# Starting addresses of the on-chip tiles in a two-block transformer kernel: transposed activations and weight buffers moved to multiples of 2048 bytes

## The chip, the cores and the metric

The kernel runs on one core of a Trainium2 chip. The metric is the device time of one execution in microseconds; three executions of the kernel before took 1178.62, 1178.98 and 1180.39 us (median 1178.98). The profile is that of one further execution, whose span from the first to the last instruction is 1177.9 us.

The engines are named as the profile names them: PE is the matrix engine (PEld its weight loads), DVE the vector engine, ACT the scalar engine, POOL GpSimd, SP the engine that issues most DMAs. In a matmul of this kernel the *stationary* operand is the activation tile (128 partitions x 128 columns, loaded before the matmul by a weight load) and the *moving* operand is a tile of weights (128 partitions x 512 columns, in some places 256) that streams past it.

## The reference, cut to what matters

Two transformer blocks in float32 over 256 tokens of width 1024: a first block of two layers (differential attention with a context, then multiscale pooling, each followed by a gated feed-forward net), and a second block (gated linear attention and block attention side by side, an MLP, a gated per-token embedding). Nearly all of the time goes to products of an activation by a weight matrix:

```
def swiglu(h, w_in, w_out):
    g, u = jnp.split(h @ w_in, 2, axis=-1)
    return (jax.nn.silu(g) * u) @ w_out
...
    h = rms_norm(x, norm_mix[i])
    u = h @ w_in[i]                                    # 1024 x 8208
    ...
    x = x + y @ w_out[i]
    h2 = rms_norm(x, norm_mlp[i])
    x = x + jnp.square(jax.nn.relu(h2 @ w_up[i])) @ w_down[i]
```

## The kernel before, in words

**Split products.** A product in float32 is made of three products in the matrix engine's one-pass format (float32r). An operand x is written as a rounded part `hi` and the rest `lo`; the product is act_hi x w_hi + act_hi x w_lo + act_lo x w_hi. So each weight block of 128 x 1024 float32 (`raw`, 512 KB, one DMA, L256) becomes two tiles: ACT writes `hi` (L286) and DVE writes `lo` = raw - hi (L292). Activations are kept transposed, k on the partitions, in two tiles each: `xTh`/`xTl` (128 x 8 x 256, the normalised input of every projection, of the gate and up products and of several output products), and others with the same role in places: `xa`/`s` (the context, k by 256 tokens), `hh`/`hl` (the hidden values of the feed-forward nets and the MLP, for the down products), `obT`/`qkd` (in the second block).

**The loops.** `mmN` (L377 to L379) runs a whole output tile of 128 tokens x 512 columns: for each of 8 k-steps three matmuls, hi x xTh, lo x xTh, hi x xTl, all into one bank. `mmK` (L391, L393) does the same for one k and two column halves, so each stationary tile meets two moving halves; `mmK_tail` (L404 to L406) is its last part. Some products stay in plain float32 (`raw` as the moving operand directly, for instance L385 and L497).

**What sets the order.** The order is written by hand, engine by engine. The class `Stream` walks one list of all weight blocks (`plan`): a DMA is issued as soon as one of the 8 `raw` buffers is free, a block is split into one of 8 `hi` and 8 `lo` buffers as soon as a pair is given back by `done`, and `done` is called when PE has used the block. Blocks of kind "m" in the same list are the 80 modulation blocks, which DVE alone reduces (L270).

**Where tiles lie.** A `Pool` hands out bytes in each partition in the order in which tile names are first asked for; pools that are opened later lie above. Pool `cp` is the lowest and holds, in this order, `prm` (parameters), `cst` (identity and tables), `xTh`, `xTl`, `mc0`, `mc1`, `half`, `crow`, and then small tiles; pool `rg` above it holds 8 `raw`, 8 `hi`, 8 `lo`; everything else is above `rg`. A tile's address therefore depends on the sizes of all tiles below it. PSUM tiles are in pool `pp` and are not touched.

Of the kernel before, what the change touches and what calls it, by code (L numbers as in the profile page):

```python
# [18 lines left out]
P = 128  # L19
# [144 lines left out]
CST_W = _o  # L164
# [9 lines left out]
def body(ctx: ExitStack, tc: tile.TileContext, wst, prm, cst, cst2, poolp, xT_d, cT_d, x_d, head, lam_d,  # L174
# [23 lines left out]
    cp = Pool("cp")  # L198
    ctx.callback(cp.close)
    rg = Pool("rg")  # L200
# [4 lines left out]
    def big():  # L205
        return pp.t([P, 1024], "big")
# [14 lines left out]
        return cp.t([P, w], f"st{w}", bufs=8)  # L221

    prm_s = cp.t([P, PRM_W], "prm")
    cst_s = cp.t([P, CST_W], "cst")
    xTh = cp.t([P, KD, T], "xTh", F32R)
    xTl = cp.t([P, KD, T], "xTl", F32R)
    mc = [cp.t([P, 48], f"mc{l}") for l in range(2)]
    half_e = cp.t([P, 8], "half")
    crow = cp.t([P, D], "crow")
    G.memset(half_e, -0.5)  # L230

    def prmc(n):
# [196 lines left out]
            A.activation(dh, ps, AF.Copy, scale=scale)  # L429
            V.scalar_tensor_tensor(dl, ps, scale, dh.bitcast(F32), op0=OP.mult, op1=OP.subtract)  # L430

    # ---------------------------------------------------------------- block 1, layer 0: projections
    b1 = Pool("b1")
    hch = b1.t([P, KD, T], "xa", F32R)
    hcl = b1.t([P, KD, T], "s", F32R)
# [215 lines left out]
            q_transposes(qr[tt - 2], tt - 2)  # L651
    a1.close()

    # ---------------------------------------------------------------- layer 0: differential attention
    a2 = Pool("a2")
    ss, ssum, ops, state, osb, rr = {}, {}, {}, {}, {}, {}

# [145 lines left out]
    for i in range(n_it + 5):  # L803
# [30 lines left out]
        if i >= 5 and items[i - 5][1] % 4 == 3:  # L834
            t, f = items[i - 5][0], items[i - 5][1] // 4
# [3 lines left out]
    a2.close()  # L839
    at.close()  # L840

    # ---------------------------------------------------------------- block 1: residual stream
    pw = []

    br = Pool("br")
# [231 lines left out]
    cur["grow"] = s[1]  # L1077
    linK8("WO", olh, wo_mid, core(0), wo_t0, core(1), wps[0])

    # ---------------------------------------------------------------- layer 0 ffn  # L1080
    nx = {}

    def mid_g2c():
# [57 lines left out]

    ffn(0, fp, x_t(1), ac0(0), mid_pool, ac0(1), {XM: mid_xa, 2: mid_g2c, 3: mid_g2r, 4: mid_gb, 5: mid_gbr})

    # ---------------------------------------------------------------- layer 1: multiscale pool
    pps = [big()]

    def res(t):
# [51 lines left out]
    st.hold = False  # L1199
    st.pump()  # L1200

    # ---------------------------------------------------------------- layer 1 ffn
    def mid1_c():
        nx["g2c"] = mcol(1, 5)
        nx["rows"] = ln_rows(3, 1.0)
# [34 lines left out]

    ffn(1, fp, x_t(1), ac1(0), lambda: None, after1_1, {XM: mid_xa, 4: mid1_c, 5: mid_g2r})

    # ---------------------------------------------------------------- block 2: projections
    hx.clear()
    state = {}
    fp.close()
# [59 lines left out]
        if i >= 2:  # L1306
            qk_tr()

    # ---------------------------------------------------------------- block 2: causal attention with distance bias
    mo_o = {}  # L1310
    mo_sum = {}
    mo_st = {}
# [60 lines left out]
    per = -(-len(steps) // 9)  # L1373
# [17 lines left out]
        steps.pop(0)()  # L1391
    mo.close()

    # ---------------------------------------------------------------- block 2: gated linear attention
    g2 = Pool("g2")
    obT = [g2.t([P, KD, T], f"obT{i}", F32R) for i in range(2)]
    for t in range(2):
# [131 lines left out]
    for i, (c, t) in enumerate(seq):  # L1529
        f = int(c[2])  # L1530
# [29 lines left out]
            g_fin(0)  # L1560
    g_fin(1)

    # ---------------------------------------------------------------- block 2: gated branches and output projection
    yT = [g2.t([P, KD, T], "obT0", F32R), g2.t([P, KD, T], "qkd", F32R)]
    for i, (f, t) in enumerate([(0, 0), (1, 0), (0, 1), (1, 1)]):
        sl = slice(512 * f, 512 * f + 512)
# [18 lines left out]
    gl.close()  # L1585
    fp = Pool("fp3")

    # ---------------------------------------------------------------- block 2: mlp
    J = DMLP // 512
    hs, hT = {}, {}  # L1590
    ops_ = [big(), big()]
# [58 lines left out]
            down(j, 1, True)  # L1650
            rcore(1)(ops_[1])

    # ---------------------------------------------------------------- block 2: gated per-token embedding
    st.hold = False
    st.pump()
    for i, (f, t) in enumerate([(0, 0), (1, 0), (0, 1), (1, 1)]):
# [117 lines left out]
```

## Time and profile before

| | before |
|---|---|
| median of 3 executions (range) | 1178.98 us (1178.62 to 1180.39) |
| span of the profiled execution | 1177.9 us |
| PE busy, share of the span | 1132.6 us, 96% |
| DVE busy | 761.6 us, 65% |
| ACT busy | 559.7 us, 48% |
| weights and inputs read | 232.63 MB, 198 GB/s over the span |

The busy time of PE is made of modelled matmul lengths, which overlap one another in time: a matmul of 512 columns is given some 390 to 400 ns, though the next one starts about 230 ns after it. The cost of a matmul in a dense run is therefore read from the distance between starts in the timeline, and the modelled length serves only to compare one group with another.

### The profile page before, as it was taken

The page shows a single profiled execution, that of the slowest core. Times are in us where ns is not written, and L with a number is a line of the kernel's source. Part 1 is how long each engine was busy: PE and PEld are TensorE (multiplying, and loading weights), DVE is VectorE, ACT ScalarE, POOL GpSimd, SP SyncE. Part 2 cuts the span into 40 slices and gives each one's busy share as a digit, 9 for nine tenths or more (in the row PEclk, how much of TensorE's full clock was granted, in tenths as well). Part 3 has the DMA queues.
Part 4 walks back from the last instruction along what each step waited for, and adds up shares of the span by engine and source line. Part 5 has one row for each costly group of instructions (what it writes and reads, how often), then busy time and mean ns, then how long its engine had stood idle before and what let it go on. Part 6 is the DMA issues. An engine that isn't in the chain of part 4 may idle for free. (4 is left out here: it accounts for less than half of the span.)

```text
span 1177.9 us, 14166 instructions
## 1 busy us (share of the span) xinstructions
PE 1132.6 (96%) x5186; PEld 883.1 (75%) x5186; DVE 761.6 (65%) x1114; ACT 559.7 (48%) x913; POOL 22.6 (2%) x35
## 2 busy tenths in 40 slices
PE   7989988899999999999999999989999999999998
PEld 3568665578888776888887687877768877888877
DVE  7978868768886674577446765454545775455555
ACT  3552456454344426534444755457235464444453
POOL 0000000000000000000000110000000000000000
PEclk9999999999999999999999999999999999999999
DMA  9877713658897705568463755442343645554521
GB/s 339 308 273 254 280 68 134 234 204 332 304 396 256 277 29 204 205 212 295 172 219 127 234 187 172 153 166 93 140 143 136 218 147 183 174 195 166 210 91 36
DMA packets 65922, 234.62 MB, mean 199 GB/s; under 512 B 7323, under 2 KB 8347, under 8 KB 65852
## 3 DMA queue, kind: packets, MB, share of 16 engines
q1 hardware_dynamic: 63936, 227.84, 54.7%
q10 hardware_dynamic: 1916, 5.87, 1.5%
q8 instruction: 41, 0.67, 0.2%
q14 instruction: 29, 0.24, 0.1%
HBM read 232.63 MB, written 1.05 MB: 198 GB/s over the span
## 5 line engine op out<-in xcount | busy, mean ns | idle before, releaser
L292 DVE TENSOR_TENSOR lo<-raw,hi 128x1024 fp32r<-128x1024 f32 x316 | 375.0, 1220 | 129.1 <-ACT hi L286 126.5
L286 ACT ACTIVATE hi<-raw 128x1024 fp32r<-128x1024 f32 x316 | 323.2, 1057 | 110.3 <-PE mm L379 61.0
L377 PE MATMUL mm<-hi,xTh 128*128 128x512 f32 (+1 forms) x872 | 343.3, 394 | 6.7 <-ACT xTh L426 3.9
L379 PE MATMUL mm<-hi,xTl 128*128 128x512 f32 (+1 forms) x872 | 338.0, 388 | 2.0 <-DVE xTl L427 1.6
L378 PE MATMUL mm<-lo,xTh 128*128 128x512 f32 (+1 forms) x872 | 337.9, 388 | 1.1 <-DVE lo L292 1.1
L377 PEld LDWEIGHTS mm<-hi,xTh 128*128 128x128 f32 x872 | 165.2, 190 | 48.1 <-ACT xTh L426 5.9
L379 PEld LDWEIGHTS mm<-hi,xTl 128*128 128x128 f32 x872 | 164.9, 189 | 40.2 <-DVE xTl L427 3.3
L378 PEld LDWEIGHTS mm<-lo,xTh 128*128 128x128 f32 x872 | 165.3, 190 | 36.5 <-DVE lo L292 2.3
L270 DVE SCALAR_TENSOR_TENSOR raw<-raw,crow 128x1024 f32<-128x1024 f32 x80 | 96.5, 1217 | 0.5 <-DMA raw<-in_dram 0.5
L391 PE MATMUL big<-hi,hh 128*128 128x512 f32 x256 | 80.8, 397 | 0.0
L391 PE MATMUL big<-lo,hh 128*128 128x512 f32 x256 | 79.2, 391 | 0.0
L393 PE MATMUL big<-hi,hl 128*128 128x512 f32 x256 | 79.1, 390 | 0.0
L426 ACT ACTIVATE hh<-tr 128x512 fp32r<-128x512 f32 (+1 forms) x40 | 23.0, 575 | 87.2 <-PE tr L983 44.4
L427 DVE TENSOR_TENSOR hl<-tr,hh 128x512 fp32r<-128x512 f32 (+1 forms) x40 | 26.3, 660 | 50.4 <-ACT hh L426 49.7
L391 PEld LDWEIGHTS big<-lo,hh 128*128 128x128 f32 x256 | 48.1, 188 | 10.4
L393 PEld LDWEIGHTS big<-hi,hl 128*128 128x128 f32 x256 | 48.1, 188 | 10.4
L963 ACT ACTIVATE h<-mm 128x512 f32<-128x512 f32 (+1 forms) x24 | 13.5, 562 | 86.5 <-PE mm L379 86.4
L391 PEld LDWEIGHTS big<-hi,hh 128*128 128x128 f32 x256 | 46.7, 188 | 8.7
L421 POOL TENSOR_TENSOR st<-st,half 128x4 f32<-128x4 f32 (+1 forms) x28 | 21.7, 776 | 1056.3 <-DVE st L419 1043.1
L1600 DVE TENSOR_TENSOR h<-h 128x512 f32<-128x512 f32 x16 | 11.0, 688 | 34.7 <-ACT h L1599 34.7
L971 DVE TENSOR_TENSOR h<-h,mm 128x512 f32<-128x512 f32 (+1 forms) x24 | 15.3, 638 | 21.8 <-PE mm L379 21.8
L1599 ACT ACTIVATE h<-mm 128x512 f32<-128x512 f32 x16 | 9.6, 598 | 39.4 <-PE mm L379 39.4
(316 smaller groups left out, 1252.1 us busy)
## 6 DMA issues: line engine op xcount, KB each, us to landing
raw<-in_dram SPq DMA_DIRECT2D x426, 512.0 KB, 5.3
row<-in_dram ACTq DMA_DIRECT2D x8, 512.0 KB, 6.3
tok<-in_dram SPq DMA_DIRECT2D x8, 256.0 KB, 7.1
xa<-in_dram SPq DMA_DIRECT2D x2, 512.0 KB, 5.1
out_dram<-sg SPq DMA_DIRECT2D x3, 256.0 KB, 2.0
pmat<-in_dram ACTq DMA_DIRECT2D x1, 544.0 KB, 11.1
crow<-in_dram ACTq DMA_DIRECT2D x1, 512.0 KB, 5.1
out_dram<-sg SPq DMA_DIRECT2D x2, 128.0 KB, 1.7
```

The source lines that it names most:

```text
L270: V.scalar_tensor_tensor(raw, raw, 1.0, crow, op0=OP.mult, op1=OP.mult, accum_out=mc[l][:, nb:nb + 1])
L286: A.activation(hi, raw, AF.Copy)
L292: V.tensor_tensor(lo, raw, hi.bitcast(F32), op=OP.subtract)
L377: TE.matmul(ps, h, hi[:, sl], start=s, stop=False)
L378: TE.matmul(ps, h, lo[:, sl], start=False, stop=False)
L379: TE.matmul(ps, l, hi[:, sl], start=False, stop=e)
L391: TE.matmul(halves[f], h, w[:, f * 512:(f + 1) * 512], start=first and b == 0, stop=False)
L393: TE.matmul(halves[f], l, hi[:, f * 512:(f + 1) * 512], start=False, stop=last)
L421: G.tensor_tensor(r, v, half_e[:, :w], op=OP.pow)
L426: A.activation(dh, ps, AF.Copy)
L427: V.tensor_tensor(dl, ps, dh.bitcast(F32), op=OP.subtract)
L971: V.tensor_tensor(h[:, :w], h[:, :w], ps[:, :w], op=OP.mult)
```

## The change

Only the order and the sizes of tiles in the two lowest pools change:

```
     prm_s = cp.t([P, PRM_W], "prm")
-    cst_s = cp.t([P, CST_W], "cst")
+    mc = [cp.t([P, 48], f"mc{l}") for l in range(2)]
+    half_e = cp.t([P, 184], "half")[:, :8]
     xTh = cp.t([P, KD, T], "xTh", F32R)
     xTl = cp.t([P, KD, T], "xTl", F32R)
-    mc = [cp.t([P, 48], f"mc{l}") for l in range(2)]
-    half_e = cp.t([P, 8], "half")
+    cst_s = cp.t([P, CST_W], "cst")
     crow = cp.t([P, D], "crow")
+    raw0 = rg.t([P, 368], "pad")
     G.memset(half_e, -0.5)
```

In the other hunks a comment line is replaced by an empty line. `mc0`, `mc1` and `half` go below `xTh`, `half` is made 736 bytes long of which the first 32 are used as before, `cst` goes above `xTl`, and an unused tile of 1472 bytes is put below the weight buffers. The starts that result, in bytes from the beginning of a partition, from the two built programs:

| tile | start before | remainder by 256 / by 2048 | start after | remainder by 256 / by 2048 |
|---|---|---|---|---|
| `xTh` | 18656 | 224 / 224 | 18432 | 0 / 0 |
| `xTl` | 26848 | 224 / 224 | 26624 | 0 / 0 |
| `cst` | 17312 | 160 / 928 | 34816 | 0 / 0 |
| `crow` | 35456 | 128 / 640 | 36160 | 64 / 1344 |
| `raw`, first of 8 | 40832 | 128 / 1920 | 43008 | 0 / 0 |
| `hi`, first of 8 | 73600 | 128 / 1920 | 75776 | 0 / 0 |
| `lo`, first of 8 | 106368 | 128 / 1920 | 108544 | 0 / 0 |
| `xa` | 139136 | 128 / 1920 | 141312 | 0 / 0 |
| `s` | 147328 | 128 / 1920 | 149504 | 0 / 0 |
| `hh0`, one of its places | 204928 | 128 / 128 | 207104 | 0 / 256 |
| `obT0` | 181632 | 128 / 1408 | 183808 | 0 / 1536 |

Everything from the weight buffers upwards moves by the same 2176 bytes. On all five engines the instructions, their order and the semaphores that they wait for are the same in the two programs, and each weight block goes through the same one of the eight buffers.

## Rows read from the trace of the kernel before

**Rows 1.** The page's first part: busy us (share of the span), instructions.
```profile
PE 1132.6 (96%) x5186; PEld 883.1 (75%) x5186; DVE 761.6 (65%) x1114; ACT 559.7 (48%) x913; POOL 22.6 (2%) x35
```
**Rows 2.** Waits of PE from 240 us on: us, times, longest.
```profile
PE mm L377 <- ACT xTh L426: 2.6, 3, 1.8
PE tr L1431 <- DMA gst<-in_dram: 1.9, 1, 1.9
...
PE mm L377 <- ACT xTh L738: 0.2, 1, 0.2
```
**Rows 3.** Waits of ACT from 240 us on: us, times, longest.
```profile
ACT h L963 <- PE mm L379: 86.4, 21, 5.2
ACT hi L286 <- PE mm L379: 61.0, 69, 10.9
...
ACT hi L286 <- DMA raw<-in_dram: 29.1, 14, 5.3
```
**Rows 4.** PE groups by shape: modelled busy us, mean ns of one, idle before.
```profile
L379 PE MATMUL mm<-hi,xTl 128*128 128x512 f32 x792 | 315.5, 398 | 2.0 <-DVE xTl L427 1.6 <-DVE xTl L740 0.4
L378 PE MATMUL mm<-lo,xTh 128*128 128x512 f32 x792 | 315.5, 398 | 1.1 <-DVE lo L292 1.1
...
L391 PE MATMUL big<-lo,hh 128*128 128x512 f32 x256 | 79.2, 391 | 0.0
...
L377 PE MATMUL mm<-hi,xTh 128*128 128x256 f32 x80 | 22.6, 283 | 0.0
...
L378 PE MATMUL mm<-lo,xa 128*128 128x512 f32 x32 | 12.5, 390 | 0.0
```
**Rows 5.** Timeline of PE in the value projection: start us, us, line.
```profile
103.12 0.39 PE L377 MATMUL mm<-hi,xa 128*128 128x512 f32 x1
...
108.57 0.39 PE L377 MATMUL mm<-hi,xTh 128*128 128x512 f32 x1
...
114.18 1.04 PE L606 MATMUL tr<-cst,tok 128*128 128x128 f32 x8
```
**Rows 6.** Timeline of PE in the feed-forward net of layer 1.
```profile
500.25 0.62 PE L391 MATMUL big<-hi,hh 128*128 128x512 f32 x2
...
505.70 0.60 PE L983 MATMUL tr<-cst,h 128*128 128x128 f32 x4
...
512.77 0.39 PE L377 MATMUL mm<-hi,xTh 128*128 128x512 f32 x1
...
529.63 0.40 PE L377 MATMUL mm<-hi,xTh 128*128 128x512 f32 x1
```
**Rows 7.** Two stretches, instructions with xTh alone: us, busy (x) by engine, PEclk.
```profile
0.00:240.00 240.00, 63.09 (x207) 39.10 (x208) 6.16 (x12) 5.99 (x12) 0.99 0.67 238
240.00:1178.00 938.00, 511.76 (x1674) 305.78 (x1673) 19.65 (x58) 18.95 (x58) 1.00 0.54 189
```
**Rows 8.** The same with xTl alone.
```profile
0.00:240.00 240.00, 36.64 (x103) 19.59 (x103) 6.16 (x12) 0.99 0.67 238
240.00:1178.00 938.00, 323.11 (x838) 157.53 (x837) 19.65 (x58) 1.00 0.54 189
```
**Rows 9.** Timeline of PE: pieces of plain float32 products, four and four.
```profile
40.52 1.88 PE L497 MATMUL mm<-raw,tok 128*128 128x512 f32 x4
42.24 1.88 PE L497 MATMUL tr<-raw,tok 128*128 128x512 f32 x4
```
**Rows 10.** Stretches of 10 us: PE, PEld, DVE, ACT, POOL busy, PEclk, DMA share, GB/s.
```profile
70.00:80.00 10.00, 9.82 (x36) 7.87 (x37) 9.45 (x16) 4.17 (x6) 0.00 (x0) 0.83 0.56 197
190.00:200.00 10.00, 8.39 (x52) 6.23 (x53) 8.99 (x22) 8.36 (x25) 1.01 (x1) 1.00 0.17 56
330.00:340.00 10.00, 10.00 (x79) 9.66 (x78) 9.74 (x13) 6.35 (x10) 0.00 (x0) 1.00 1.02 409
```
**Rows 11.** The page's costliest groups: the two splits; busy us, mean ns, idle before.
```profile
L292 DVE TENSOR_TENSOR lo<-raw,hi 128x1024 fp32r<-128x1024 f32 x316 | 375.0, 1220 | 129.1 <-ACT hi L286 126.5
L286 ACT ACTIVATE hi<-raw 128x1024 fp32r<-128x1024 f32 x316 | 323.2, 1057 | 110.3 <-PE mm L379 61.0
```

## The prediction, on record before the changed kernel ran

> **What bounds the kernel now.** I read the shares first, then the waits, then the timeline. PE is busy for 96% of the span, DVE for 65%, ACT for 48% [rows 1]. A busy share proves little with overlapping modelled lengths, so the waits come next. From 240 us on, PE waits for anybody in 24 places only, 14.0 us together; the rows show the two longest of the sixteen groups and the last [rows 2]. ACT in the same stretch waits for PE: 86.4 us before L963 and 61.0 us before a weight split, for PE to give a buffer back [rows 3]. So over four fifths of the span the pace is that of PE's own matmuls, and a nanosecond on each of them is a nanosecond on the clock. Before 240 us it is mixed: from 190 to 200 us PE works 8.39 of 10 us while DVE, at 8.99, and ACT, at 8.36, carry the softmax [rows 10].
>
> The change issues the same instructions, so the only question is whether an operand's start changes an instruction's length. The trace of before holds its own experiment on that. `xTh`/`xTl` begin 224 past a multiple of 256 (and of 2048); each of their 128-column slices is 512 bytes long, so all slices begin 32 bytes past a multiple of 64. `xa`, `s`, `hh`, `hl`, `obT` and `qkd` play the same part in the same lines of code, and begin 128 past a multiple of 256, all slices on multiples of 64. In the value projection the context tokens use `xa`/`s` and the others `xTh`/`xTl`, against the same weight tiles, from the same three lines. The last 24 matmuls with `xa`/`s` take 103.12 to 108.57, 227.1 ns each; the next 24, with `xTh`/`xTl`, take 108.57 to 114.18, 233.8 ns each [rows 5]. In the feed-forward net 24 matmuls with `hh`/`hl` take 500.25 to 505.70, 227.1 ns each, and soon after 72 with `xTh`/`xTl` 512.77 to 529.63, 234.2 ns each [rows 6]. The modelled lengths of whole groups agree: 398 ns with `xTh` against 390 with `xa` and 391 with `hh` [rows 4]. So the groups with the odd start pay 6.7 to 7.1 ns more, nearly 3%. I take 6.7, from the pair with the same weights and lines.
>
> **The change, part by part.**
> *The start of xTh and xTl.* After it the slices begin on multiples of 512. I expect the spacing that `xa` has, 227 ns. How many matmuls: 1674 with `xTh` and 838 with `xTl` after 240 us, 207 and 103 before [rows 7, 8]; some 2820 in all, of the 4056 split products of the program. Of those after 240 us, 240 have 256 columns (80 of each of three lines, one shown [rows 4]) and 16 have `xTh` or `xTl` moving, which leaves 2256 with 512 columns.
> - 2256 x 6.7 ns = 15.1 us.
> - 240 short ones: no row shows a short one with the other start. Bounds: nothing, or the full 6.7 ns each, 1.6 us. I take 0.7.
> - 310 before 240 us: at most 2.1 us, at least nothing where DVE sets the pace; I take half, 1.0.
> - Against it stand the waits. Where PE waits for a chain of ACT and DVE that its own earlier matmul started, the matmuls that cover the chain shrink and the wait grows by as much. The cover is one output tile of 24 matmuls in most places, so 24 x 6.7 = 0.16 us at each of the 24 places [rows 2], at most 3.9 us, at least 0. I take 2.0.
> Sum: 15.1 + 0.7 + 1.0 - 2.0 = 14.8 us. The profiled span is 1177.9 and the median 1178.98, so 1.1 us lie outside the span; they stay. 1178.98 - 14.8 = **1164.2**, rounded to 1164. By the ends of the terms it is 1160.2 (15.1 + 1.6 + 2.1) to 1167.8 (15.1 - 3.9).
>
> *The start of weight buffers and of everything above.* These go from 128 past a multiple of 256 to a multiple of 256, the weights to one of 2048, all by the same 2176 bytes, so nothing changes between them. ACT's and DVE's splits and the DMA see the other start too. No row shows any of them at a multiple of 256, so the price has two ends. A gain is possible only down to what the array needs: four pieces of a plain float32 product, 512 columns each, take 40.52 to 42.24, 430 ns apiece [rows 9]. A split product streams its columns faster than that; half of 430, 215 ns, is an estimate of the least it could take, and 227.1 - 215 = 12.1 ns on each split product is the far end. For a loss the nearest row is the 6.7 ns of `xTh` itself. I take nothing: the plain products show no loss at these same `raw` starts, and the splits of ACT and DVE, 1.06 and 1.22 us a block [rows 11], lie beside the 12 matmuls that a block of 512 KB feeds for two token tiles, 12 x 227 = 2.7 us. If a split grew by a few per cent it would still hide after 240 us; before it, where DVE sets the pace in places, 1% of its time is at most 2 us. The DMA reached 409 GB/s with the old starts while PE stayed full [rows 10].
>
> *cst, crow, the small tiles.* The identity `cst` is a moving operand of transposes, the small tiles belong to the LN chains. Their instruction counts are a few hundred; at the 7 ns of the only difference seen, under 2 us, and I take nothing for it.
>
> **The rivals.**
> *No difference.* The 7 ns belong to something else that `xTh`/`xTl` have and `xa` has not, such as the place in memory (18 to 35 KB against 139 KB and up); then they stay, and the time is 1179. For it: the trace has no copy of `xTh` at another start. Against it: `xa` and `hh` lie 34 KB apart or more and agree on 227, and `xTh` differs from both by the same amount.
> [...]
>
> *More than xTh.* The start on a multiple of 256 or 2048 also takes part of the remaining 12.1 ns off every split product. There are 4056 of them (2820 and 1236 with the other tiles), so half of it would be 25 us more, 1139, and all of it 49 us, 1115. For it: 227 is above 215. Against it: neither kind of stationary tile comes near 215 in a row with split products, so the half of a plain product may say nothing on them.
> [...]
>
> *Slower.* With the new layout the stationary slices of `xTh`, the moving weights, what ACT and DVE write and what the DMA fills all begin on multiples of 2048 or 512, where now `xTh` is off by 1696 from the weights. If streams that begin in step get in one another's way, every split product pays. The place is the dense runs of lines 377 to 379 and 391 to 393. At the 6.7 ns seen between two starts, the 1236 good ones lose 8.3 us and the others gain nothing: 1187. It turns slower as soon as the price is over 14.8 us / 4056 = 3.6 ns a matmul. Against it: `xa` and the weights both begin at 1920 of 2048 now, in step, and run at 227.1 [rows 5].
>
> *Gain absorbed.* A faster PE asks for weights 3% faster. Where the DMA share is 1.02 and DVE has 9.74 of 10 us [rows 10], they could become the bound: the stretch from 260 to 350 us would give back some 2 us. With PE waiting more often than thought, up to half of the gain: 1172. Against it: PE was idle nowhere there. [...]
>
> **How the numbers follow.** As forecast, 1158 to 1168: 0.70. Gain absorbed, 1168 to 1176.6: 0.11. More than xTh, under 1158: 0.08. No difference: 0.07. Slower: 0.04. The range reaches from 1154 to 1173, taking in the likeliest case, a small part of the extra gain and most of the absorbed one. A measurement of this kernel tells 0.2%, 2.4 us, from no change: faster is 0.70 + 0.11 + 0.08 = 0.89, same 0.07, slower 0.04.
>
> **What would show it.** In the changed kernel's timeline the 24 matmuls with `xTh` in the value projection take 5.45 us instead of 5.61, and those with `hh` the same 5.45 as now. The mean of L378 falls from 398 to about 390 ns. The splits keep their lengths. The waits of PE after 240 us grow by less than 4 us. I am wrong in the term of `xTh` if its runs stay at 234, in the second term if runs with `hh` leave 227, and in the last if PE's waits grow by more than 4 us.

## The result and the profile after

| | before | after |
|---|---|---|
| median of 4 executions each (range) | 1178.8 us (1176.28 to 1180.39) | 1164.16 us (1161.51 to 1166.95) |
| ratio, 95% interval | | 0.9878 (0.986 to 0.9896) |
| span of the profiled execution | 1177.9 us | 1165.2 us (its own time 1166.95) |

The changed kernel is 1.2% faster, 14.6 us. In its line numbers everything from the pad on is one higher: L377 to L379 of before are L378 to L380, L391 is L392.

The first part of the page after, the answer to [rows 1] (busy us, share, instructions):

```profile
PE 1120.5 (96%) x5186; PEld 884.0 (76%) x5186; DVE 761.2 (65%) x1114; ACT 560.0 (48%) x913; POOL 22.7 (2%) x35
```

Only PE's busy time has moved, by 12.1 us; DVE, ACT and the loads of stationary tiles (PEld) have kept theirs within 0.9 us. The groups of PE by shape, which answer [rows 4] (modelled busy us, mean ns of one, idle before):

```profile
L380 PE MATMUL mm<-hi,xTl 128*128 128x512 f32 x792 | 311.4, 393 | 2.0 <-DVE xTl L428 1.6 <-DVE xTl L741 0.4
L379 PE MATMUL mm<-lo,xTh 128*128 128x512 f32 x792 | 310.8, 392 | 1.9 <-DVE lo L293 1.9
...
L392 PE MATMUL big<-lo,hh 128*128 128x512 f32 x256 | 79.2, 391 | 0.0
...
L378 PE MATMUL mm<-hi,xTh 128*128 128x256 f32 x80 | 22.9, 286 | 0.5 <-ACT h L964 0.5
...
L379 PE MATMUL mm<-lo,xa 128*128 128x512 f32 x32 | 12.5, 390 | 0.0
```

The two groups of 792 with `xTh` and `xTl` fell from 398 to 392 and 393 ns, those with `hh` and `xa` stayed at 391 and 390, and the short ones of 256 columns rose from 283 to 286. The distance between starts says it without a model. PE's timeline in the value projection, which answers [rows 5] (start us, us, line):

```profile
100.99 0.39 PE L378 MATMUL mm<-hi,xa 128*128 128x512 f32 x1
...
106.43 0.39 PE L378 MATMUL mm<-hi,xTh 128*128 128x512 f32 x1
...
111.88 1.03 PE L607 MATMUL tr<-cst,tok 128*128 128x128 f32 x8
```

24 matmuls with `xa`/`s` take 5.44 us as before; the 24 with `xTh`/`xTl` now take 5.45 where they took 5.61. In the feed-forward net of layer 1, against [rows 6]:

```profile
495.37 0.62 PE L392 MATMUL big<-hi,hh 128*128 128x512 f32 x2
...
500.81 0.60 PE L984 MATMUL tr<-cst,h 128*128 128x128 f32 x4
...
508.57 0.39 PE L378 MATMUL mm<-hi,xTh 128*128 128x512 f32 x1
...
524.89 0.39 PE L378 MATMUL mm<-hi,xTh 128*128 128x512 f32 x1
```

The 24 with `hh`/`hl` take 5.44 us, 226.7 ns each, and the 72 with `xTh`/`xTl` 16.32 us, 226.7 ns each, where they took 16.86. The waits of PE in the same stretch as [rows 2] (from 238 us on, since the same work now begins some 2 us sooner):

```profile
PE mm L378 <- ACT xTh L427: 2.7, 3, 1.8
PE mm L379 <- DVE lo L293: 1.9, 4, 0.7
...
PE tr L1432 <- DMA gst<-in_dram: 1.6, 1, 1.6
...
PE mm L378 <- ACT h L964: 0.5, 1, 0.5
```

All 17 groups together make 15.5 us in 26 places, 1.5 more than before. The splits, against [rows 11]:

```profile
L293 DVE TENSOR_TENSOR lo<-raw,hi 128x1024 fp32r<-128x1024 f32 x316 | 374.6, 1220 | 126.2 <-ACT hi L287 121.8
L287 ACT ACTIVATE hi<-raw 128x1024 fp32r<-128x1024 f32 x316 | 323.1, 1057 | 106.6 <-PE mm L380 56.8
```

They keep 1220 and 1057 ns. One part of the difference between the two profiled executions is not the change's. Stretches of 10 us of the kernel after in which the granted clock is below one, from 240 us on (PE, PEld, DVE, ACT, POOL busy, PEclk, DMA share, GB/s):

```profile
440.00:450.00 10.00, 7.58 (x29) 4.94 (x28) 7.82 (x10) 9.15 (x17) 0.54 (x1) 0.92 0.94 339
450.00:460.00 10.00, 10.00 (x45) 8.20 (x45) 4.33 (x6) 5.32 (x10) 0.55 (x1) 0.91 0.56 195
780.00:790.00 10.00, 8.43 (x40) 5.33 (x39) 3.73 (x6) 6.35 (x10) 0.00 (x0) 0.82 0.52 169
790.00:800.00 10.00, 10.00 (x43) 8.22 (x42) 2.13 (x4) 8.82 (x11) 0.00 (x0) 0.84 0.09 35
```

And of the kernel before, in the same places:

```profile
450.00:460.00 10.00, 9.28 (x32) 7.10 (x33) 5.48 (x8) 8.19 (x14) 0.54 (x1) 0.83 0.80 293
790.00:800.00 10.00, 8.08 (x37) 5.39 (x36) 3.81 (x5) 6.14 (x10) 0.00 (x0) 0.85 0.42 160
```

An estimate of what the clock takes is 10 us times what is missing to one: 0.8 + 0.9 + 1.8 + 1.6 = 5.1 us after, 1.7 + 1.5 = 3.2 before (3.4 with the 0.2 of the next stretch). The profiled execution after lies 2.8 us above its median, and the mean granted clock is not the same in all executions of one kernel: after, it is 0.991 in three of the four, the profiled one among them, and 0.995 in the fourth, the shortest (1161.51 us). In the profile of `f2_pad_96`, below, no stretch of 10 us from 240 to 1150 us is under 1.00.

### The profile page after: what moved, and what is told of

Read it like the earlier page. It is cut to its first block, busy times and chain, and to the rows that moved or that the text cites. A ratio compares the mean times of both kernels' runs of the same rounds, so it can differ in the third digit from the quotient of the medians.

```text
span 1165.2 us, 14166 instructions
## 1 busy us (share of the span) xinstructions
PE 1120.5 (96%) x5186; PEld 884.0 (76%) x5186; DVE 761.2 (65%) x1114; ACT 560.0 (48%) x913; POOL 22.7 (2%) x35
## 5 line engine op out<-in xcount | busy, mean ns | idle before, releaser
L293 DVE TENSOR_TENSOR lo<-raw,hi 128x1024 fp32r<-128x1024 f32 x316 | 374.6, 1220 | 126.2 <-ACT hi L287 121.8
L287 ACT ACTIVATE hi<-raw 128x1024 fp32r<-128x1024 f32 x316 | 323.1, 1057 | 106.6 <-PE mm L380 56.8
L378 PE MATMUL mm<-hi,xTh 128*128 128x512 f32 (+1 forms) x872 | 339.7, 390 | 7.3 <-ACT xTh L427 4.0
L380 PE MATMUL mm<-hi,xTl 128*128 128x512 f32 (+1 forms) x872 | 334.0, 383 | 2.0 <-DVE xTl L428 1.6
L379 PE MATMUL mm<-lo,xTh 128*128 128x512 f32 (+1 forms) x872 | 333.4, 382 | 1.9 <-DVE lo L293 1.9
L378 PEld LDWEIGHTS mm<-hi,xTh 128*128 128x128 f32 x872 | 165.4, 190 | 45.0 <-ACT xTh L427 5.9
L380 PEld LDWEIGHTS mm<-hi,xTl 128*128 128x128 f32 x872 | 165.1, 189 | 36.1 <-DVE xTl L428 3.3
L379 PEld LDWEIGHTS mm<-lo,xTh 128*128 128x128 f32 x872 | 165.6, 190 | 33.5 <-DVE lo L293 3.4
L392 PE MATMUL big<-hi,hh 128*128 128x512 f32 x256 | 80.6, 396 | 0.0
L392 PE MATMUL big<-lo,hh 128*128 128x512 f32 x256 | 79.2, 391 | 0.0
L392 PEld LDWEIGHTS big<-lo,hh 128*128 128x128 f32 x256 | 48.0, 188 | 10.3
L392 PEld LDWEIGHTS big<-hi,hh 128*128 128x128 f32 x256 | 46.7, 188 | 8.6
```

What stands on the lines that cost most here:

```text
L287: A.activation(hi, raw, AF.Copy)
L293: V.tensor_tensor(lo, raw, hi.bitcast(F32), op=OP.subtract)
L378: TE.matmul(ps, h, hi[:, sl], start=s, stop=False)
L379: TE.matmul(ps, h, lo[:, sl], start=False, stop=False)
L380: TE.matmul(ps, l, hi[:, sl], start=False, stop=e)
L392: TE.matmul(halves[f], h, w[:, f * 512:(f + 1) * 512], start=first and b == 0, stop=False)
```

## The experiments

**The theories.** *A, the prediction's:* the stationary tile's own start matters; 32 past a multiple of 64 is bad. *B:* the multiples of 2048 that the change makes are what is good. *C:* neither start matters by itself, only the difference between the start of the stationary slice and that of the moving weights, by 256. In the kernel before, `xa`, `hh`, `hl`, `s` and `obT` have the remainder 128 by 256, and so have the weights; `xTh` has 224. After, all have 0. So the two kernels can't tell A, B and C apart.

All kernels compute the whole result; only starts differ. In the table the starts are remainders by 256, the differences are stationary minus moving, by 256, and the spacing is the median distance from the start of a 512-column matmul to the next start on PE (in the line numbers of the kernel after: the 792 of line 379 with `lo` and `xTh`; the 256 of line 392 with `lo` and `hh`), with the range of the middle eight tenths.

| kernel | start xTh / weights / hh, xa | difference xTh | ns | difference hh, xa | ns | time, us | ratio (95%) |
|---|---|---|---|---|---|---|---|
| before | 224 / 128 / 128 | 96 | 234 (231 to 238) | 0 | 227 | 1178.8 | |
| after | 0 / 0 / 0 | 0 | 227 (226 to 231) | 0 | 227 | 1164.16 | 0.9878 (0.986 to 0.9896) |
| `e1_xt_only` | 0 / 128 / 128 | 128 | 232 (229 to 241) | 0 | 227 | 1174.46 | 0.9968 (0.9954 to 0.9983) |
| `e2_weights_only` | 224 / 0 / 0 | 224 | 234 (231 to 235) | 0 | 227 | 1174.01 | 0.9969 (0.9953 to 0.9984) |
| `e3_all_64` | 64 / 64 / 64 | 0 | 227 (226 to 231) | 0 | 227 | 1165.4 | 0.9889 (0.986 to 0.9918) |
| `e4_xt_32` | 32 / 0 / 0 | 32 | 232 (231 to 235) | 0 | 227 | 1174.85 | 0.9976 (0.9964 to 0.9989) |
| `f2_pad_96` | 224 / 224 / 224 | 0 | 227 (226 to 228) | 0 | 227 | 1166.47 | 0.9905 (0.988 to 0.9931) |
| `g1_off_64_32` | 0 / 192 / 224 | 64 | 233 (231 to 236) | 32 | 233 (231 to 235) | 1181.99, one run | |
| `g2_off_16_192` | 16 / 0 / 192 | 16 | 235 (231 to 235) | 192 | 231 (229 to 232) | 1177.07, one run | |
| `h1_off_160_128` | 0 / 96 / 224 | 160 | 232 (231 to 238) | 128 | 231 (228 to 238) | 1184.26, one run | |
| `h2_off_192_64` | 0 / 64 / 128 | 192 | 226 (225 to 232) | 64 | 233 (231 to 236) | 1170.38, one run | |

The ratios are to the kernel before on the same chip, 1178.3 us for the `e` kernels and 1177.98 for `f2`; the single runs stand beside 1177.98 (`g1`, `g2`) and 1177.78 (`h1`, `h2`). In `g2` `xTl` is not at the difference of `xTh` but at 80.

**xTh alone on its new start.** Against the changed kernel the pad is 128 bytes shorter, so that the weights and all above keep the remainder 1920 by 2048 that they had before:

```
-    raw0 = rg.t([P, 368], "pad")
+    raw0 = rg.t([P, 336], "pad")
```

> xTh and xTl begin on multiples of 2048 as in the changed kernel; weight buffers and everything above keep their old remainder, 1920 by 2048 for the weights. Theory A (the start of the stationary slice alone decides): 24 matmuls with xTh in the value projection take 5.45 us, the time is that of the changed kernel, 1164 us, within 3. Theory B (the weight buffers' start on a multiple of 2048 has a share): the spacing with xTh stays above 227 ns, and the time lies between 1164 and 1179.

PE's timeline of `e1_xt_only` in the value projection:

```profile
101.61 0.39 PE L378 MATMUL mm<-hi,xa 128*128 128x512 f32 x1
...
107.05 0.40 PE L378 MATMUL mm<-hi,xTh 128*128 128x512 f32 x1
...
112.64 1.03 PE L607 MATMUL tr<-cst,tok 128*128 128x128 f32 x8
```

24 with `xa` in 5.44 us, 24 with `xTh` in 5.59, 232.9 ns each. `xTh` begins on a multiple of 2048 and all slices of both operands on multiples of 64, and it is still slow. Theory A, on which the prediction rests, falls here: the start of `xTh` alone brings 3.8 us of the 14.6.

**The weights alone on their new start.** The kernel before with a pad:

```
     crow = cp.t([P, D], "crow")
+    raw0 = rg.t([P, 544], "pad")
```

> Weight buffers and everything above begin as in the changed kernel, weights on multiples of 2048; xTh and xTl stay at 224 past one, cst, mc and half stay as before. Theory A: spacing with xTh 234 ns, with hh and xa 227 ns, time 1179 us, within 3. Theory B: below 1176.

The value projection's 24 with `xTh` took 5.59 us here too, and the time is 1174.01: the spacing is as A expected, the time is not (1179, within 3) and is what B expected. At the full clock, and without the distances above 260 ns, the mean distance of the 512-column matmuls with `xTh`/`xTl` is 233.2 ns against 234.0 before, which over some 2500 of them is 2 us; the short ones are 117 ns apart in the median against 119, 0.5 us more. Where the rest comes from is not shown (the interval of the ratio is 1.9 to 5.5 us). Neither half of the change does what the whole does: 3.8 and 3.7 us (by the ratios) against 14.4.

**Everything 64 past the new starts.** Against the changed kernel:

```
-    half_e = cp.t([P, 184], "half")[:, :8]
+    half_e = cp.t([P, 200], "half")[:, :8]
```

> The changed kernel with everything from xTh upwards 64 bytes higher: xTh, xTl, raw, hi, lo, xa and s begin 64 past a multiple of 2048, none on a multiple of 128. Theory A with 64 bytes as the grain: nothing changes, spacing 227 ns, 1164 us. If the grain is 128 bytes or more: 234 ns on all 4056 split products, so 1164 + 4056 x 6.7 ns = 1191 us.

5.44 us for the 24 with `xTh`, 0.9889 by time. With `xTh` and the weights on no multiple of 128 the whole gain is there, so theory B falls.

**xTh 32 past the weights.** `xTh` and `xTl` are cut from tiles that are 8 floats longer, against the changed kernel:

```
-    xTh = cp.t([P, KD, T], "xTh", F32R)
-    xTl = cp.t([P, KD, T], "xTl", F32R)
+    xTh = cp.t([P, KD * T + 8], "xTh", F32R)[:, 8:8 + KD * T].rearrange("p (k t) -> p k t", t=T)
+    xTl = cp.t([P, KD * T + 8], "xTl", F32R)[:, 0:0 + KD * T].rearrange("p (k t) -> p k t", t=T)
...
-    raw0 = rg.t([P, 368], "pad")
+    raw0 = rg.t([P, 352], "pad")
```

> The changed kernel with xTh and xTl alone 32 bytes higher (32 past a multiple of 2048); weight buffers and everything above them as in the changed kernel, cst and crow 64 higher. Theory A: spacing with xTh back at 234 ns, time 1178 us. If the place in memory or something about 224 decided and not the remainder by 64: 227 ns, 1164 us.

32 bytes of difference cost about as much as 96, 128 or 224: 5.60 us for the 24, 1174.85 in time, 3 us under what A expected. The spacing agrees with A as well as with C; it tells only that the difference need not be large.

**In step, on odd starts.** The experiment that decides between A and C. The kernel before with 96 bytes of padding below the weight buffers and no other edit; `xTh` stays on its old start, 32 past a multiple of 64, and the weights and all above move to the same remainder, off the multiples of 64:

```
     crow = cp.t([P, D], "crow")
+    raw0 = rg.t([P, 24], "pad")
```

> The kernel before with one unused tile of 96 bytes below the weight buffers and nothing else: xTh, xTl, the weight buffers, xa, s, hh, hl, obT and qkd all begin 224 past a multiple of 256, none on a multiple of 64. Theory C (a split product takes 227 ns where the stationary and the moving operand begin with the same remainder by 256, and 232 to 235 where not): spacing 227 ns with every tile, time 1164 us, within 3. Theory A (the start of the stationary slice by 64 decides): 234 ns with every tile, all 4056 split products, 1178.3 + 1236 x 6.7 ns = 1187 us. By multiples of 2048: 1178 or above.

PE's timeline of `f2_pad_96` in the value projection:

```profile
102.19 0.39 PE L378 MATMUL mm<-hi,xa 128*128 128x512 f32 x1
...
107.63 0.39 PE L378 MATMUL mm<-hi,xTh 128*128 128x512 f32 x1
...
113.08 1.03 PE L607 MATMUL tr<-cst,tok 128*128 128x128 f32 x8
```

The `xTh` tile at the start that the prediction called the cause runs at 227.1 ns. The intervals of `f2`, `e3` and after overlap, so 96 bytes buy the whole gain as far as these few executions can tell. By 512 the starts differ by 256 here (the weights at 40928, remainder 480, `xTh` at 18656, remainder 224), and the tile is fast, so in these kernels the period is 256, not 512; nor is it 128, since `e1`, 128 apart, takes 232 ns.

**The good ones put out of step.** Against the changed kernel the first pad is 64 bytes shorter, and a second one of 32 bytes above `lo` takes `xa`, `hh`, `hl`, `obT` out of step with the weights for the first time:

```
-    raw0 = rg.t([P, 368], "pad")
+    raw0 = rg.t([P, 352], "pad")
...
+            if self.pad2 is None:
+                self.pad2 = rg.t([P, 8], "pad2")
```

> The changed kernel with the weight buffers 64 bytes lower and all tiles above them 32 bytes lower than it has them: by 256, xTh and xTl begin 64 after the weights, hh, hl, xa, s, obT and qkd 32 after them. Theory C: both groups lose, spacing 232 to 235 ns for xTh and, for the first time, for hh and xa too; 1164 + 4056 x 6 ns = 1188 us. Theory A: hh and xa 234 (they begin 32 past a multiple of 64), xTh 227 ns.

PE's timeline of `g1_off_64_32` in the value projection (L381 to L383 are the same three lines):

```profile
101.83 0.40 PE L381 MATMUL mm<-hi,xa 128*128 128x512 f32 x1
...
107.43 0.40 PE L381 MATMUL mm<-hi,xTh 128*128 128x512 f32 x1
...
113.03 1.04 PE L610 MATMUL tr<-cst,tok 128*128 128x128 f32 x8
```

Both runs of 24 take 5.60 us. The tiles that were at 227 ns in every kernel so far are at 233, though `xTh` has its new start and the weights lie on multiples of 64. The one execution took 1181.99 us, above the kernel before but under the 1188 that was expected.

**More differences.** As `g1`, with other lengths: `xTh` cut 16 bytes into its tile, pads of 336 and 48 floats (`g2`); pads of 392 and 32 (`h1`); pads of 384 and 16 (`h2`).

> The changed kernel with xTh and xTl 16 bytes past a multiple of 64 and all tiles above the weight buffers 192 bytes higher, weight buffers as in the changed kernel: by 256, xTh and xTl begin 16 after the weights, hh, hl, xa, s, obT and qkd 192 after them. Theory C: 232 to 235 ns for both groups, 1188 us. Theory A: hh and xa 227 ns (multiples of 64), xTh 234 ns.

> xTh and xTl begin on a multiple of 2048, the weight buffers 96 past a multiple of 256 (so xTh is 160 off by 256 from them), and a second unused tile of 128 bytes above the weight buffers puts hh, hl, xa, s and obT 128 past the weights' remainder. Both differences come from other starts than the same differences had before. Theory C (the difference by 256 decides, not the operand or its place): hh and xa at difference 128 behave as xTh did at 128 in the run with xTh alone moved: median 232 ns, spread 229 to 241, where they had 227; xTh at 160, not tried yet, is over 229. Time: 1236 matmuls with 5 ns more than before is 6 us, xTh unchanged or up to 4 us better: 1176 to 1185. Theory A (the stationary tile's own start; xTh on a multiple of 2048 is good): xTh at 227 and the time near 1170. A rule that only knows in step and out of step, with one price for every difference: hh at 234, no wide spread.

> As the last, with the weight buffers 64 past a multiple of 256 and hh, hl, xa, s, obT 128 past one: the remainder by 256 that these had in the kernel before, where they took 227 ns. Theory A (the stationary tile's own start): hh and xa stay at 227, and xTh on a multiple of 2048 is good too; time near 1164. Theory C: hh and xa are 64 off from the weights and take what xTh took at 64, 233 ns, spread 231 to 236; xTh at 192 takes 229 to 235; time 1177 to 1185, above before. The 256-column matmuls with xTh, 113 ns at a difference of 64 and 117 at 224, are under 120 at 192.

`h2` turns the old pair round: `xa` and `hh` have the remainder 128 that they had before, when they took 227 ns, and only the weights' remainder differs. The groups by shape of `h2_off_192_64`:

```profile
L381 PE MATMUL mm<-hi,xTh 128*128 128x512 f32 x792 | 317.3, 401 | 6.8 <-ACT xTh L430 4.0 <-ACT aT L689 1.5 <-ACT mv L1381 1.1
L382 PE MATMUL mm<-lo,xTh 128*128 128x512 f32 x792 | 309.9, 391 | 1.4 <-DVE lo L296 0.7 <-DVE mqs L1266 0.6
L395 PE MATMUL big<-lo,hh 128*128 128x512 f32 x256 | 80.4, 395 | 0.0
L382 PE MATMUL mm<-lo,xTh 128*128 128x256 f32 x80 | 22.2, 277 | 0.0
L382 PE MATMUL mm<-lo,xa 128*128 128x512 f32 x32 | 12.7, 395 | 0.0
```

`hh` and `xa` at 395 where they had 391 and 390, and by starts 233 ns with the middle eight tenths from 231 to 236, exactly what `xTh` takes at the same difference in `g1`. In `h1` `hh` at 128 takes 231 (228 to 238) where `xTh` took 232 (229 to 241) in `e1`: the same difference from other starts, in other tiles and lines, costs about the same, and `h1`'s 1184.26 us is above the kernel before, as expected. The expected time of `h2`, 1177 to 1185, was missed; it is 1170.38. One reason is that 192 is a mild difference: `lo` with `xTh` mostly takes 226, under the expected 229 to 235, and `hi` with `xTh` 232. `g2` shows the same for `xa` at 192 (228.8 ns over the 24 of the value projection, as 229.6 for `xTh` in `h2`), so its expectation failed in the spacing of `hh` and `xa` (232 to 235 expected, 229 to 231 measured) and in the time (1188 expected, 1177.07 measured). So the rule "out of step costs 6 ns" is too simple for one of the nine differences tried.

**The writers of the weight tiles as a rival.** In every kernel `raw`, `hi` and `lo` move together, so the difference in the table is also the difference to tiles that the DMA, ACT and DVE are filling. The trace of before speaks against these writers as the cause. Here is a stretch of it in which DVE and ACT do nothing (columns as in [rows 10]):

```profile
356.20:360.70 4.50, 4.50 (x21) 3.63 (x20) 0.00 (x0) 0.00 (x0) 0.00 (x0) 1.00 0.22 85
```

and PE's timeline there:

```profile
356.12 0.40 PE L378 MATMUL mm<-lo,xTh 128*128 128x512 f32 x1
...
360.80 0.40 PE L377 MATMUL mm<-hi,xTh 128*128 128x512 f32 x1
```

These are 20 matmuls in 4.68 us, 234 ns each. Over the whole trace, at the full clock and without the distances above 260 ns, the median with `xTh`/`xTl` is 234 ns where neither DVE nor ACT works (538 distances), where both work throughout (647), and where no DMA packet begins from 3 us before the matmul to its end (261). After the change it is 227 in all three cases. So of what the difference could mean, PE's own two operands are left.

**What the runs settle, and what not.** A product of 512 columns in this kernel takes 227 ns where the stationary slice and the moving weights begin with the same remainder by 256, whatever that is (0, 64, 128 and 224 were tried), and 226 to 235 in the median, mostly 231 to 235, at the differences 16, 32, 64, 80, 96, 128, 160, 192 and 224. Nothing tried is faster than in step throughout. Why the chip does this is not shown. The places where the tile changes give a hint of whose start counts. In `e2` and `e4` a matmul whose own slice is in step, but which stands directly before one with `xTh`, takes 235 ns in five places of five each (a sixth has a wait in it), in `e1` 232 or 233; that points at the slice of the next matmul. In the kernel before such a matmul takes only 228 or 229, so it stays a hint.

## Why the prediction was right on the time and wrong on the cause

**The term of xTh, 15.1 us: size right, cause wrong.** The spacing went from 234 to 227, as said. The distances from the starts of the 3 x 792 matmuls of L377 to L379 (some of them before 240 us) to the next starts sum to 571.4 us before and 559.3 after, 12.1 less, in an execution that lost, by the estimate above, 1.7 us more to the clock from 240 us on; in the profiles of `e3_all_64` and `f2_pad_96` they sum to 15.8 and 16.8 less. But the step that named the cause, "`xTh`/`xTl` begin 224 past a multiple of 256 [...] all slices begin 32 bytes past a multiple of 64", failed: `e1` takes that start away and keeps 232 ns, `f2` keeps that start and has 227. The pair in [rows 5] differs in two things, the stationary's own start and its distance from the weights, and I read only the first, though the table of starts had both columns: `xa` 128, `raw`, `hi` and `lo` 128, `xTh` 224.

**The start of the weights, taken at nothing.** For the splits, 1220 and 1057 ns, the plain products, 429 ns apart in every kernel, and the products with `hh` this was right, and for the reason given: all of these move together. It was wrong as a step by itself. Without the weights' move (`e1`) 3.8 us of the gain are left, so some 11 us hang on the edit that was priced at nothing. The total came out because the change happens to move both halves to one remainder; for the working as it stands that was luck. Had the change moved `xTh` alone, the same working would have said 1164 and the chip 1174.5.

**The short ones, a gain of 0.7: wrong sign.** The 240 matmuls of 256 columns went from 119 ns apart to 120 in the median, a loss of some 0.2 us. They follow another order than the long ones (medians of the three lines): 113 to 114 at 64 (`g1`) and at 192 (`h2`), 117 at 224 (`e2`), 118 to 124 at 160 (`h1`), 120 at 0 in three kernels; `h2` was expected under 120 and is. It is inside the bounds of 0 to 1.6 by size only; the loss was excluded without a reason.

**Before 240 us, 1.0.** The 24 of the value projection gave back 0.16 us, so the price of one is right there too. What reached the end isn't separable: from 60 to 150 us the mean granted clock of the two profiled executions is 0.96 before and 0.94 after, which by the same estimate, in stretches of 10 us, is 3.5 us against 5.1.

**The waits, -2.0.** They grew by 1.5 us (by 0.8 and 0.5 in the profiles of `e3` and `f2`), in the place that the prediction named: small waits for ACT's and DVE's chains (L293 from 1.1 to 1.9 us), while the one for a DMA shrank.

**The rivals.** *Slower* had the operands and the place right, and the sign turned round: streams that begin in step are the good ones here (227 ns), and its own argument against it, `xa` and the weights both at 1920 and fast, was the theory that now stands. *No difference* fell: `xTh` lies at 18432 where it lay at 18656, nearly the same place in memory, and its spacing went from 234 ns to 227. *More than xTh* fell: no group of split products with 512 columns has a median under 226 ns in any of the kernels. Its floor of 215 was half of a piece of 430; the four pieces in [rows 9] belong to two plain products, two pieces each (L497 has 80 records for 40 products), so nothing ties half a piece to a split product. *Gain absorbed* has next to nothing: PE's waits grew by 1.5 us in all, and in `f2` the span fell by 17.3 us (1177.9 to 1160.6) where the distances fell by 16.8.

## What to carry to other kernels

Compare the start of the stationary slices with that of the moving tiles, by 256, before asking whether either is "aligned" by itself; here one pad of 96 bytes between two pools was worth 1% of the kernel, and a layout with both on round numbers and another remainder (`e1`) was worth a third of that. When a trace offers a pair that differs in the wanted way, write down everything in which the two differ, the other operand's address too, and give each its own kernel. Where products are short (256 columns here), measure again, since the order was another: 113 to 119 ns in the median at the differences 64, 96, 192 and 224, 118 to 124 at 160, and 120 at none.

## What was not expected of the hardware

**At the lower clock the start cost nothing.** In both kernels the granted clock falls to 0.50 shortly after the end of a wait of PE near 790 us: before, 2.2 us after it and for 3.4 us; after the change, 1.3 us after it and for 6.8 us. PE's timeline before, where `xTh` is 96 out of step:

```profile
797.34 0.63 PE L379 MATMUL mm<-hi,xTl 128*128 128x512 f32 x1
...
799.47 0.63 PE L378 MATMUL mm<-lo,xTh 128*128 128x512 f32 x1
```

and after, in step:

```profile
788.09 0.63 PE L379 MATMUL mm<-lo,xTh 128*128 128x512 f32 x1
...
792.36 0.63 PE L380 MATMUL mm<-hi,xTl 128*128 128x512 f32 x1
```

with the granted clock in a microsecond of the first:

```profile
798.00:799.00 1.00, 1.00 (x3) 0.76 (x3) 0.00 (x0) 0.99 (x3) 0.00 (x0) 0.50 0.28 66
```

and in one of the second:

```profile
790.00:791.00 1.00, 1.00 (x4) 0.79 (x3) 0.13 (x1) 1.00 (x1) 0.00 (x0) 0.50 0.81 332
```

At 0.50, 5 distances before take 2.13 us, 426 ns each, and 10 after take 4.27, 427 each. Over the whole traces the median distance with `xTh`/`xTl` at 0.50 is 427 ns in both kernels (22 distances before, 31 after). The difference of 7 ns is there at the full clock alone (234 against 227 ns); why is not shown.

**The loads took as long as before.** The loads of the stationary tile keep their 190 ns, before and after (busy us, mean ns, idle before):

```profile
L378 PEld LDWEIGHTS mm<-lo,xTh 128*128 128x128 f32 x872 | 165.3, 190 | 36.5 <-DVE lo L292 2.3 <-issue 0.2
...
L379 PEld LDWEIGHTS mm<-lo,xTh 128*128 128x128 f32 x872 | 165.6, 190 | 33.5 <-DVE lo L293 3.4 <-issue 0.2
```

The mean granted clock of the profiled executions is 0.993 before and 0.991 after, so it brings none of the gain. What moves is the distance between matmuls, by 2 to 3%, and with it the whole kernel, by 1.2%.
